# Loading half B's x^T in 320-column pieces, its decay products behind dense ones, cache set-up queued late, and half A's residual tiles at memory's other end, in a two-layer hybrid encoder step

## The chip, the cores and the metric

The kernel runs on one core of one Trainium2 chip. Its engines work side by side and each takes its own instructions in a fixed order: TensorE (PE, matrix products; PEld in the profile is its weight loading), VectorE (DVE), ScalarE (ACT), GpSimd (POOL) and SyncE (SP), which issues nearly all DMAs here. The metric is the device time of the program in microseconds (us). All arithmetic is fp32; a value x that enters a product is split into a rounded part hi and a rest lo, and a product is made as hi·hi + hi·lo + lo·hi, three matmuls.

## What is computed

The reference is one inference step of two layers over 1024 prompt frames and 64 sample frames of width 1024. Layer 0 projects x to the inputs of two mixers, a recurrent one (RWKV-7, 8 heads) and gated linear attention (GLA, 4 heads); layer 1 is chunk-band softmax attention that also reads a K/V cache of 128 rows. After each follow a layer norm, a SwiGLU channel mixer and another layer norm.

```python
for layer in range(DEPTH):
    if layer % 2 == 0:
        p = x @ P['w_in_mix'][e]
        ya, wkv, sh = rwkv7_time_mix(p[..., :A_PROJ], ...)
        yb, gs = gla_mix(p[..., A_PROJ:], gla0[e], P['b_alpha_up'][e], P['b_alpha_bias'][e], P['b_norm_w'][e])
        mix = jnp.concatenate([ya, yb], axis=-1) @ P['w_out_mix'][e]
    else:
        mix, kr, vr = chunk_band_attention(x, P['c_w_qkv'][o], P['c_rel_bias'][o], P['c_w_o'][o], ck, cv)
    x = layer_norm(DEEPNORM_ALPHA * x + mix, P['ln1_w'][layer], P['ln1_b'][layer])
    x = layer_norm(DEEPNORM_ALPHA * x + swiglu(x, P['ffn_w_in'][layer], P['ffn_w_out'][layer]), ...)
```

In gla_mix the decay is `log_sigmoid(xa @ alpha_up + alpha_bias) / 16`, where xa is 16 columns of the projection p.

## The kernel before

**Halves.** The tokens are cut in half A (hf = 0: 384 prompt frames and the 64 sample frames, 448 columns) and half B (hf = 1: the other 640 prompt frames). x is held transposed (x^T), as eight k tiles of 128 rows by the half's columns, each hi and lo.

**Order.** `run` (L1337) traces the program in an order; a scheduler then makes each engine's fixed order from it by a clock of its own: of the instructions that could go, the one traced first. So what is traced later serves as filler. Layer 0 runs like this: half A's input projection (`inproj_rwkv(0)`, `inproj_gla(0)`), then half A's recurrences (`rwkv(0)` and `gla(0)`, the scan below: many small matmuls and long chains of small DVE operations), with half B's input projection traced behind them, so that its dense products fill PE; then half B's scan, with half A's output projection, layer norm and ffn as filler.

**Half B's x^T.** At L1370 `xt_tiles_in` makes its tiles: the first three k tiles lie in tiles of their own (names xeh and xel, in a pool on the right end of memory), the other five lie over half A's x^T (names xh and xl), so they can be written only when half A's input projection has read what was there. `load_xt(1)` (L1371) loads each k tile [128, 640] into a buffer xraw of the tag wr, which has two buffers and is the one that all weights are loaded into (`load_w`, L94), casts it on ACT (L215) and subtracts on DVE or, for odd k tiles, POOL (L216). With a pool as argument, `load_xt` takes raw tiles yraw from that pool (tag yr, 8 buffers) instead; half A's loads do this with the pool yp.

**The projection of GLA.** `inproj_gla` (L339) first makes the decays: two loads (L344, L357), 16 products of 32 columns for each segment (L352, weights xaw), their evacuation (L355), then the up-projection (L363) and its functions, stored at L369. After that come four dense products for q and k (L370 to L377, each with 24 matmuls for each segment by `gemm_ws`, L124 to L126), then v (L382 to L388) and the gate (L389 to L397). Half B has two segments of 320 columns, half A one of 448.

**Memory.** Pools are stacked from the left or the right end. On the left, `yr` and `one` (buffers of the input projection) are closed at L1376 and L1378, and `ap` and `accA` come in their place: accA holds half A's residual tiles acc (`load_acc`, L793: four loads of 512 KB, L797) and the packed sample tile xpk (L851, L852). On the right lie the constants and the scan's pool, and on them the pool xb with xeh and xel, closed at L1376.

**Output projection of half A.** `load_xt(0, yg_d)` (L1377) reads the scans' outputs back into half A's x^T, k tile by k tile: 4 to 7 from GLA, 0 to 3 from RWKV, whose outputs y are stored at L654. `proj` (L855) multiplies first k tiles 4 to 7, then 0 to 3; the sums go to acc (L825, L827). It starts by packing the sample columns of all eight k tiles into xpk.

**Cache set-up.** `cache_setup` (L1117) is traced in half A's ffn, behind j = 8. It loads four parts of the V cache (tile cv, one buffer, L1122), casts them on ACT and subtracts on DVE (`split`, L113 and L114, tile cvh), and stores them (L1125); then the same for two parts of the K cache with a transpose on PE (L1128 to L1136). It depends on nothing before it, so the scheduler may put it anywhere earlier.

**Evacuation in the scan.** The scan's `rw1` makes three small products into the bank pa (L437 to L439), which ACT empties (L441, L443, L445); the next products pb (L484) need the same bank.

Of the kernel before, what the change touches and what calls it, by code (L numbers as in the profile page):

```python
# [20 lines left out]
NA, NB = PA + 64, 1024 - PA  # L21
NM = max(NA, NB)
# [61 lines left out]
class Kern:  # L84
# [9 lines left out]
    def load_w(self, src, shape):  # L94

        nc = self.nc
        raw = self.wp.tile(shape, F32, tag="wr", name="wr", bufs=2)
        self.last_w = nc.sync.dma_start(raw, src).ins
        hi = self.wp.tile(shape, F32R, tag="wh", name="wh", bufs=self.WB)
        lo = self.wp.tile(shape, F32R, tag="wl", name="wl", bufs=self.WB)  # L100
        self.A.copy(hi, raw)  # L101
        self.wcount += 1
        m = shape[1]
        h = m * 5 // 8 if self.both else m * (self.wcount % 2)
        if h:
            self.V.tensor_tensor(lo[:, :h], raw[:, :h], hi[:, :h].bitcast(F32), op=ALU.subtract)  # L106
        if h < m:
            self.G.tensor_tensor(lo[:, h:], raw[:, h:], hi[:, h:].bitcast(F32), op=ALU.subtract)  # L108
        return hi, lo
# [229 lines left out]
    def inproj_gla(self, hf, pool):  # L339
        nc, V, A, G, T = self.nc, self.V, self.A, self.G, self.T  # L340
        n, c0, xt = self.N[hf], self.base[hf], self.xt[hf]

        raw = pool.tile([128, 8, 16], F32, tag="xar", name="xar", bufs=1)
        nc.sync.dma_start(raw, self.a["w_xa"])  # L344
        whl = pool.tile([128, 8, 32], F32R, tag="xaw", name="xaw", bufs=1)
        A.copy(whl[:, :, 0:16], raw)
        V.tensor_tensor(whl[:, :, 16:32], raw, whl[:, :, 0:16].bitcast(F32), op=ALU.subtract)
        segs = self.banks(hf)
        for kt in range(8):
            for i, xx in enumerate((xt.h(kt), xt.l(kt))):  # L350
                for ps, s0, w in segs:
                    T.matmul(ps[0:32, :], whl[:, kt, :], xx[:, s0 : s0 + w], start=(kt + i == 0), stop=(kt + i == 8))  # L352
        xa = pool.tile([32, NM], F32, tag="xa", name="xa", bufs=1)
        for ps, s0, w in segs:
            V.tensor_copy(xa[:, s0 : s0 + w], ps[0:32, :])  # L355
        up = pool.tile([32, 256], F32, tag="up", name="up", bufs=1)
        nc.sync.dma_start(up, self.a["up2"])  # L357
        for p in range(2):
            segs = self.banks(hf)
            mn = pool.tile([128, NM], F32, tag="sq", name="mn", bufs=3)[:, :n]  # L360
            ab = pool.tile([128, NM], F32, tag="sq", name="abz", bufs=3)[:, :n]
            for ps, s0, w in segs:
                T.matmul(ps, up[:, 128 * p : 128 * p + 128], xa[:, s0 : s0 + w], start=True, stop=True)  # L363
                V.tensor_scalar(mn[:, s0 : s0 + w], ps, self.ab[:, p : p + 1], 0.0, op0=ALU.add, op1=ALU.min)
                A.activation(ab[:, s0 : s0 + w], ps, AF.Abs, bias=self.ab[:, p : p + 1])
            A.activation(ab, ab, AF.Exp, scale=-1.0)
            A.activation(ab, ab, AF.Ln, bias=self.one)
            G.tensor_tensor(ab, ab, mn, op=ALU.subtract)
            nc.sync.dma_start(self.qkl_d[2, p, :, c0 : c0 + n], ab)  # L369
        for ct in range(4):  # L370
            w = self.load_w(self.a["w_in"][14 + ct], [128, 8, 128])
            segs = self.banks(hf)
            self.gemm_ws(w, xt, segs)
            t = pool.tile([128, NM], F32, tag="t1", name="gq", bufs=2)
            for ps, s0, wd in segs:
                A.copy(t[:, s0 : s0 + wd], ps)
            nc.sync.dma_start(self.qkl_d[ct // 2, ct % 2, :, c0 : c0 + n], t[:, :n])  # L377
        ws = []
        for i in range(4):
            hi, lo = self.load_w(self.a["w_gv"][i], [128, 2, 512])  # L380
            ws += [(hi[:, 0, :], lo[:, 0, :]), (hi[:, 1, :], lo[:, 1, :])]
        for i0 in range(0, n, 128):  # L382
            m = min(128, n - i0)
            ps = self.bank()[:m]
            self.gemm_ts(ps, ws, xt.h, xt.l, list(range(8)), lambda x: x[:, i0 : i0 + m])
            t = pool.tile([128, 512], F32, tag="xs", name="gvs", bufs=2)
            A.copy(t[:m], ps)
            nc.sync.dma_start(self.gv_d[c0 + i0 : c0 + i0 + m, :], t[:m])  # L388
        for ct in range(4):  # L389
            w = self.load_w(self.a["w_in"][18 + ct], [128, 8, 128])  # L390
            segs = self.banks(hf)
            self.gemm_ws(w, xt, segs)
            t = pool.tile([128, NM], F32, tag="t1", name="grg", bufs=2)
            for ps, s0, wd in segs:
                A.activation(t[:, s0 : s0 + wd], ps, AF.Tanh, scale=0.5)
                V.scalar_tensor_tensor(t[:, s0 : s0 + wd], t[:, s0 : s0 + wd], 1.0, ps, op0=ALU.add, op1=ALU.mult)
            nc.sync.dma_start(self.sg_d[ct, :, c0 : c0 + n], t[:, :n])  # L397
# [939 lines left out]
    def run(self):  # L1337
        nc, tc, a = self.nc, self.tc, self.a
# [12 lines left out]
        yp = es_yr.enter_context(tc.tile_pool(name="yr", bufs=1))  # L1351
# [16 lines left out]
        for _ in g:  # L1368
            pass
        self.xt[1] = self.xt_tiles_in(es_one.enter_context(tc.tile_pool(name="xb", bufs=1, side="right")), 8 - NA * 8 // NB)  # L1370
        self.load_xt(1)  # L1371
        self.inproj_gla(1, one)
        self.inproj_rwkv(1, one)
        nc.sync.dma_start(a["s_shift"].rearrange("c p -> p c"), self.shS)
# [4 lines left out]

        self.ap = self.ctx.enter_context(tc.tile_pool(name="ap", bufs=1))  # L1380
        es_a = ExitStack()
        pa = es_a.enter_context(tc.tile_pool(name="accA", bufs=1))
        acc0 = self.load_acc(0, a["x"], pa)
        xd = lambda hf: (lambda t0, m: self.x_d[self.base[hf] + t0 : self.base[hf] + t0 + m, :])
        gS = []
# [16 lines left out]
        for j in self.ffn(0, 0, acc0, hp, lambda: self.layer_norm(0, acc0, "ln2", 0, xd(0))):  # L1402
            if j == 6:
                self.bias_setup(hp)
            if 12 <= j < 20:
                for h in range(2 * j - 24, 2 * j - 22):
                    self.bias_copies(h)
            if j == 8:
                with tc.tile_pool(name="as", bufs=1) as asp:
                    self.cache_setup(asp)  # L1410
        for p in range(4):
            self.wkv_out(sc, S[p], a["p_wkv"][2 * p : 2 * p + 2])
# [32 lines left out]
        accA = self.ctx.enter_context(tc.tile_pool(name="accA1", bufs=1, side="right"))  # L1445
# [7 lines left out]
        es_a = ExitStack()  # L1453
# [135 lines left out]
```

## Time and profile before

| what | us |
|---|---|
| median of 3 runs | 3117.12 |
| lowest, highest | 3116.71, 3119.89 |
| profiled execution | 3121.6 |
| its span, first to last instruction | 3119.8 |
| half B's x^T: first and last load issued | 151.3, 175.6 |
| V cache parts: first and last load issued | 532.0, 578.1 |
| K cache parts: loads issued | 584.9, 1005.8 |
| half A's residual tiles: first load issued | 562.3 |

In a row of stages stand the stretch and its length in us, then each engine's busy time with its instructions in brackets (PE, PEld, DVE, ACT, POOL, as far as they are asked for), then the granted clock of TensorE as a share of full speed, the share of time that the DMA engines are busy, and GB/s. A row of the order of time has start, duration, engine, line, operation, out<-in by the program's names, shapes and the number of instructions merged; in square brackets stands how long the engine was idle before it, and what ended that. SPq stands for DMAs that SP issues. A row of waits tells who waited for whom: sum in us, times, longest.

### The profile page before, as it was taken

The page shows a single profiled execution, that of the slowest core. Times are in us where ns is not written, and L with a number is a line of the kernel's source. Part 1 is how long each engine was busy: PE and PEld are TensorE (multiplying, and loading weights), DVE is VectorE, ACT ScalarE, POOL GpSimd, SP SyncE. Part 2 cuts the span into 40 slices and gives each one's busy share as a digit, 9 for nine tenths or more (in the row PEclk, how much of TensorE's full clock was granted, in tenths as well). Part 3 has the DMA queues.
Part 4 walks back from the last instruction along what each step waited for, and adds up shares of the span by engine and source line. Part 5 has one row for each costly group of instructions (what it writes and reads, how often), then busy time and mean ns, then how long its engine had stood idle before and what let it go on. Part 6 is the DMA issues. An engine that isn't in the chain of part 4 may idle for free. (4 is left out here: it accounts for less than half of the span.)

```text
span 3119.8 us, 50045 instructions
## 1 busy us (share of the span) xinstructions
PE 3017.0 (97%) x17468; PEld 2676.2 (86%) x17468; DVE 2021.3 (65%) x4941; ACT 1272.0 (41%) x2761; POOL 1363.5 (44%) x1489
## 2 busy tenths in 40 slices
PE   9999999899999999999999999999999989899998
PEld 7788888688888887888999899899999978799987
DVE  4677875879898764455554466245666667766567
ACT  4454554344454323233443132345444433333332
POOL 2354534444454333443332233244555555745444
PEclk9989999889999999999999999999999999999999
DMA  6554334533533228444343232866455443322222
GB/s 201 140 155 119 108 109 123 141 105 109 137 110 112 89 97 274 140 134 123 116 133 105 81 95 98 247 201 182 126 150 145 132 160 107 116 80 95 67 82 75
DMA packets 298492, 399.29 MB, mean 128 GB/s; under 512 B 125504, under 2 KB 218552, under 8 KB 298240
## 3 DMA queue, kind: packets, MB, share of 16 engines
q1 hardware_dynamic: 297088, 393.48, 42.4%
q8 instruction: 138, 2.26, 0.3%
q10 hardware_dynamic: 1152, 2.62, 0.2%
q14 instruction: 114, 0.93, 0.1%
HBM read 323.63 MB, written 75.51 MB: 128 GB/s over the span
## 5 line engine op out<-in xcount | busy, mean ns | idle before, releaser
L108 POOL TENSOR_TENSOR wl<-wr,wh 128x512 fp32r<-128x512 f32 (+2 forms) x297 | 521.7, 1760 | 642.1 <-ACT wh L101 592.3
L124 PE MATMUL gps<-xh,wh 128*128 128x320 f32 (+1 forms) x2188 | 746.0, 341 | 7.8 <-ACT xh L215 5.9
L125 PE MATMUL gps<-xl,wh 128*128 128x320 f32 (+1 forms) x2188 | 745.0, 340 | 0.6 <-DVE xl L216 0.6
L126 PE MATMUL gps<-xh,wl 128*128 128x320 f32 (+1 forms) x2188 | 744.3, 340 | 0.9 <-DVE wl L106 0.9
L101 ACT CAST wh<-wr 128x1024 fp32r<-128x1024 f32 x360 | 375.8, 1048 | 457.3 <-PE gps L125 131.2
L106 DVE TENSOR_TENSOR wl<-wr,wh 128x512 fp32r<-128x512 f32 (+2 forms) x297 | 289.6, 975 | 248.9 <-ACT wh L101 246.0
L124 PEld LDWEIGHTS gps<-xh,wh 128*128 128x128 f32 x2188 | 414.4, 189 | 30.6 <-ACT xh L215 5.9
L126 PEld LDWEIGHTS gps<-xh,wl 128*128 128x128 f32 x2188 | 413.8, 189 | 19.9 <-DVE wl L106 2.1
L125 PEld LDWEIGHTS gps<-xl,wh 128*128 128x128 f32 x2188 | 414.0, 189 | 18.1 <-DVE xl L216 1.0
L1294 POOL TENSOR_SCALAR s<-s,mx 128x640 f32<-128x640 f32 (+5 forms) x144 | 203.9, 1416 | 272.1 <-DVE mx L1293 250.7
L135 PE MATMUL gps<-wh,xh 128*128 128x512 f32 x661 | 262.0, 403 | 6.8 <-ACT xh L1092 2.5
L138 PE MATMUL gps<-wh,xl 128*128 128x512 f32 x661 | 258.9, 399 | 6.1 <-DVE xl L216 6.1
L136 PE MATMUL gps<-wl,xh 128*128 128x512 f32 x661 | 263.0, 400 | 1.3 <-DVE wl L106 1.1
L136 PE MATMUL gps<-wl,hh 128*128 128x512 f32 x572 | 226.7, 398 | 0.3 <-DVE wl L106 0.3
L135 PE MATMUL gps<-wh,hh 128*128 128x512 f32 x572 | 226.2, 397 | 0.3 <-DVE acc L827 0.3
L827 DVE TENSOR_TENSOR acc<-acc,gps 128x512 f32<-128x512 f32 x216 | 143.6, 679 | 86.8 <-PE gps L138 83.6
L138 PE MATMUL gps<-wh,hl 128*128 128x512 f32 x484 | 189.5, 398 | 2.2 <-DVE hl L942 2.2
L549 DVE TENSOR_TENSOR t<-lt,x 16x48 f32<-16x48 f32 (+9 forms) x540 | 147.3, 273 | 35.8 <-DMA lt<-l_d 25.4
L1292 ACT ACTIVATE s<-s,mx 128x640 f32<-128x640 f32 (+5 forms) x144 | 96.4, 669 | 162.3 <-DVE mx L1291 153.8
L135 PEld LDWEIGHTS gps<-wh,xh 128*128 128x128 f32 x661 | 125.9, 191 | 37.6 <-ACT wh L101 4.3
L138 PEld LDWEIGHTS gps<-wh,xl 128*128 128x128 f32 x661 | 125.7, 190 | 34.4 <-DVE xl L216 6.9
L136 PEld LDWEIGHTS gps<-wl,xh 128*128 128x128 f32 x661 | 126.2, 191 | 30.4 <-DVE wl L106 2.7
(383 smaller groups left out, 6327.8 us busy)
## 6 DMA issues: line engine op xcount, KB each, us to landing
wr<-in_w_fi SPq DMA_DIRECT2D x176, 512.0 KB
wr<-in_w_fo SPq DMA_DIRECT2D x88, 512.0 KB
wr<-in_w_in SPq DMA_DIRECT2D x44, 512.0 KB
wr<-in_w_qk SPq DMA_DIRECT2D x32, 512.0 KB
wr<-in_w_o SPq DMA_DIRECT2D x24, 512.0 KB
qs<-qd SPq DMA_DIRECT2D x32, 320.0 KB
wr<-in_w_om SPq DMA_DIRECT2D x16, 512.0 KB
wr<-in_w_v SPq DMA_DIRECT2D x16, 512.0 KB
```

What stands on the lines that cost most here:

```text
L101: self.A.copy(hi, raw)
L106: self.V.tensor_tensor(lo[:, :h], raw[:, :h], hi[:, :h].bitcast(F32), op=ALU.subtract)
L108: self.G.tensor_tensor(lo[:, h:], raw[:, h:], hi[:, h:].bitcast(F32), op=ALU.subtract)
L124: self.T.matmul(ps, hi[:, kt, :], xh, start=(kt == 0), stop=False)
L125: self.T.matmul(ps, hi[:, kt, :], xl, start=False, stop=False)
L126: self.T.matmul(ps, lo[:, kt, :], xh, start=False, stop=(kt == nk - 1))
L135: self.T.matmul(ps, xh, wh, start=(i == 0), stop=False)
L136: self.T.matmul(ps, xh, wl, start=False, stop=(lo is None and i == n - 1))
L138: self.T.matmul(ps, cols(lo(kt)), wh, start=False, stop=(i == n - 1))
L549: V.tensor_tensor(tv, lt[:, j, w:16].unsqueeze(2).to_broadcast([m, r, w]), x[:, 0, j, 0:w].unsqueeze(1).to_broadcast([m, r, w]), op=ALU.mult)
L827: self.V.tensor_tensor(a, a, ps[:m], op=ALU.add)
L1294: G.tensor_scalar(s[:m, :nk], s[:m, :nk], mx[:m, 3:4], None, op0=ALU.mult)
```

## The change

The casts of cache set-up are given an order behind the last weight cast traced so far (`last_cast`, set in `load_w`), and the cache's loads one behind the last weight load (`last_w`): `issue_after` puts every instruction that the block traces on that instruction's engine behind it. The decay products move into a function that half A calls where they stood and half B calls behind the four q and k products. Half B's x^T is loaded in 16 pieces of 320 columns through the pool yp. The pool accA goes to the right end.

```diff
-        self.A.copy(hi, raw)
+        self.last_cast = self.A.copy(hi, raw).ins
...
     def inproj_gla(self, hf, pool):
...
+        def decay():
+            raw = pool.tile([128, 8, 16], F32, tag="xar", name="xar", bufs=1)
+            nc.sync.dma_start(raw, self.a["w_xa"])
...
+                nc.sync.dma_start(self.qkl_d[2, p, :, c0 : c0 + n], ab)
+
+        if hf == 0:
+            decay()
         for ct in range(4):
             w = self.load_w(self.a["w_in"][14 + ct], [128, 8, 128])
...
             nc.sync.dma_start(self.qkl_d[ct // 2, ct % 2, :, c0 : c0 + n], t[:, :n])
+        if hf:
+            decay()
         ws = []
...
-        self.load_xt(1)
+        for kt in range(8):
+            for c in (0, NB // 2):
+                self.load_xt(1, None, (kt,), slice(c, c + NB // 2), yp)
         self.inproj_gla(1, one)
...
-        pa = es_a.enter_context(tc.tile_pool(name="accA", bufs=1))
+        pa = es_a.enter_context(tc.tile_pool(name="accA", bufs=1, side="right"))
...
-                with tc.tile_pool(name="as", bufs=1) as asp:
+                with tc.tile_pool(name="as", bufs=1) as asp, tc.issue_after(self.last_w), tc.issue_after(self.last_cast):
                     self.cache_setup(asp)
```

The body of `decay` is what stood at the head of `inproj_gla` before, unchanged.

More of the change, by code (lines that the diff above doesn't have):

```diff
@@ L341, in inproj_gla @@
         n, c0, xt = self.N[hf], self.base[hf], self.xt[hf]
[L343 to L350, printed above, removed]
-                for ps, s0, w in segs:
-                    T.matmul(ps[0:32, :], whl[:, kt, :], xx[:, s0 : s0 + w], start=(kt + i == 0), stop=(kt + i == 8))
@@ L353, in inproj_gla @@
[L353 to L369, printed above, removed]
+        def decay():
+            raw = pool.tile([128, 8, 16], F32, tag="xar", name="xar", bufs=1)
+            nc.sync.dma_start(raw, self.a["w_xa"])
+            whl = pool.tile([128, 8, 32], F32R, tag="xaw", name="xaw", bufs=1)
+            A.copy(whl[:, :, 0:16], raw)
+            V.tensor_tensor(whl[:, :, 16:32], raw, whl[:, :, 0:16].bitcast(F32), op=ALU.subtract)
+            segs = self.banks(hf)
+            for kt in range(8):
+                for i, xx in enumerate((xt.h(kt), xt.l(kt))):
+                    for ps, s0, w in segs:
+                        T.matmul(ps[0:32, :], whl[:, kt, :], xx[:, s0 : s0 + w], start=(kt + i == 0), stop=(kt + i == 8))
+            xa = pool.tile([32, NM], F32, tag="xa", name="xa", bufs=1)
+            for ps, s0, w in segs:
+                V.tensor_copy(xa[:, s0 : s0 + w], ps[0:32, :])
+            up = pool.tile([32, 256], F32, tag="up", name="up", bufs=1)
+            nc.sync.dma_start(up, self.a["up2"])
+            for p in range(2):
+                segs = self.banks(hf)
+                mn = pool.tile([128, NM], F32, tag="sq", name="mn", bufs=3)[:, :n]
+                ab = pool.tile([128, NM], F32, tag="sq", name="abz", bufs=3)[:, :n]
+                for ps, s0, w in segs:
+                    T.matmul(ps, up[:, 128 * p : 128 * p + 128], xa[:, s0 : s0 + w], start=True, stop=True)
+                    V.tensor_scalar(mn[:, s0 : s0 + w], ps, self.ab[:, p : p + 1], 0.0, op0=ALU.add, op1=ALU.min)
+                    A.activation(ab[:, s0 : s0 + w], ps, AF.Abs, bias=self.ab[:, p : p + 1])
+                A.activation(ab, ab, AF.Exp, scale=-1.0)
+                A.activation(ab, ab, AF.Ln, bias=self.one)
+                G.tensor_tensor(ab, ab, mn, op=ALU.subtract)
+                nc.sync.dma_start(self.qkl_d[2, p, :, c0 : c0 + n], ab)
@@ L1370, in run @@
         self.xt[1] = self.xt_tiles_in(es_one.enter_context(tc.tile_pool(name="xb", bufs=1, side="right")), 8 - NA * 8 // NB)
-        self.load_xt(1)
+        for kt in range(8):
+            for c in (0, NB // 2):
+                self.load_xt(1, None, (kt,), slice(c, c + NB // 2), yp)
         self.inproj_gla(1, one)
```

## The prediction

> **What bounds the kernel now.** I read the page's totals first, then the table of stages, then, inside the two stages that lose time, the order of time of single engines.
>
> ```profile
> span 3119.8 us, 50045 instructions
> PE 3017.0 (97%) x17468; PEld 2676.2 (86%) x17468; DVE 2021.3 (65%) x4941; ACT 1272.0 (41%) x2761; POOL 1363.5 (44%) x1489
> ```
>
> PE is busy 97% of the span, so the others matter only where they hold it up, or where it runs at the lower granted clock. The table of stages (length, then busy time and instructions of each engine, then granted clock, DMA share, GB/s) shows where that is.
>
> ```profile
> 0.00:30.00 30.00, 22.64 (x87) 17.91 (x88) 13.30 (x33) 14.18 (x20) 6.57 (x11) 1.00 0.78 253
> 84.00:98.50 14.50, 11.37 (x40) 6.92 (x39) 7.58 (x25) 8.58 (x25) 6.53 (x15) 0.77 0.74 110
> 168.50:177.00 8.50, 6.96 (x50) 5.19 (x49) 4.49 (x8) 4.17 (x14) 3.37 (x6) 1.00 0.52 157
> 177.00:200.90 23.90, 23.58 (x93) 17.34 (x94) 17.86 (x62) 14.02 (x37) 15.78 (x31) 0.50 0.45 140
> 200.90:530.00 329.10, 323.21 (x2288) 287.50 (x2288) 250.35 (x896) 164.94 (x488) 139.23 (x257) 0.99 0.42 119
> 535.20:583.20 48.00, 33.16 (x150) 27.20 (x149) 32.22 (x94) 17.26 (x53) 19.58 (x30) 0.79 0.72 169
> 583.20:611.40 28.20, 28.00 (x150) 22.55 (x150) 27.83 (x69) 9.17 (x22) 12.14 (x14) 1.00 0.33 88
> 611.40:645.00 33.60, 27.70 (x135) 21.83 (x133) 29.29 (x75) 15.31 (x45) 22.74 (x29) 0.54 0.38 118
> 645.00:1160.00 515.00, 511.46 (x3091) 438.58 (x3089) 416.76 (x1273) 221.78 (x616) 225.44 (x343) 0.99 0.38 107
> 800.00:880.00 80.00, 78.89 (x503) 67.02 (x502) 68.91 (x229) 37.67 (x117) 38.58 (x63) 0.98 0.46 125
> ```
>
> Two stages stand out. From 177.0 to 200.9 PE is busy 23.58 of 23.90 us, at half clock throughout. From 535.2 to 583.2 it is busy 33.16 of 48.00 us at 0.79. Between and after them PE is nearly full at 0.99 (329.10 and 515.00 us), so a shift won in either stage should be carried through them; 611.4 to 645.0 is the layer norm of half A, where DVE has 29.29 of 33.60 us, and should move as a block.
>
> **Part one: x^T of half B, and the decay products.** The order of time on PE, and the waits of the tile xraw:
>
> ```profile
> 168.32 0.37 PE L126 MATMUL gps<-xh,wl 128*128 128x448 f32 x1
> 169.92 0.47 PE L352 MATMUL gps<-xeh,xaw 128*32 128x320 f32 x2
> 185.30 0.88 PE L352 MATMUL gps<-xl,xaw 128*32 128x320 f32 x2
> 198.11 0.64 PE L124 MATMUL gps<-xeh,wh 128*128 128x320 f32 x1
> ...
> L214 SPq DMA_DIRECT2D xraw<-in_xt x8: 333/340/432, 151.3 to 175.6; - x8
> L215 ACT CAST xh<-xraw x5: 712/725/728, 166.3 to 178.6; 128x640 fp32r<-128x640 f32 x5
>   DMA xraw<-in_xt: 10.9, 7
> ```
>
> Half A's last dense product ends at 168.7. From 169.92 PE has only the thin decay products (32 columns of the array) and the scan's small ones until the first dense one at 198.11. The decay products take from 169.92 to 186.2 because the eight loads of x^T pass two buffers that the weights also use: the last is issued at 175.6, and the casts waited 10.9 us for landings, seven times. After the change the loads have eight buffers of their own, and dense products come first. Of the 16 pieces six go to the separate tiles xeh, xel and can be split early; ten lie over half A's x^T and become writable as its last product passes (it ends at 168.7). Ten casts at half of 0.725 us are 3.6 us of ACT; the first dense segment takes 24 x 0.15 = 3.6 us (0.15 from one such matmul to the next, rows 531.47 and 531.62 further down) and the scan's products stand between, so I count no wait of PE there.
>
> The gain: 23.9 us at half clock become 12.0 if dense products are mixed in, and the idle 8.50 - 6.96 = 1.5 us go: 13.5. What comes back: the decay products still run, and half A's did so in the row 84.00:98.50, with 14.50 - 11.37 = 3.1 us idle and 0.23 x 14.5 = 3.3 us of clock. With dense v products of half B ready beside them I take 3.0 of those 6.4. **Term one: -10.5**, from -13.5 to 0.
>
> The Trainium skill (TensorE: Matmul & The Clock Gate, "What's actually happening") has full clock return after one busy window of about 3.4 us. Here PE was busy for 23.58 us and stayed at 0.50, so the trace disagrees. By that rule the slow stretch would have ended after 3.4 us whatever the products were, and mixing in dense ones would win next to nothing.
>
> Eight more issues on SP (0.34 us each) are 2.7 us among idle ones. The loads may now be issued as soon as the buffers are free, since a half-B load is issued early already:
>
> ```profile
> 31.48 0.37 SPq L344 DMA_DIRECT2D xar<-in_w_xa  x1
> ...
> PE gps L124 <- ACT wh L101: 0.9, 1, 0.9
> ```
>
> Eight pieces of 128 x 320 x 4 bytes are 1.31 MB, 5.2 us at the 253 GB/s of the first 30 us, whose DMA share is 0.78 and where PE waited 0.9 us once for a weight. **Term two: +1.0**, from 0 to 5.2, nearer to the one wait seen.
>
> The Trainium skill (DMA: Bandwidth & Descriptors, "Rules for kernel authors") wants 1 MiB or more per DMA and speaks against pieces of 160 KB. No row here prices a piece of that size; eight in flight should hide it.
>
> **Part two: cache set-up out, residual tiles on the right.** The order of time of SP, ACT, DVE and PE, and one row of SP's waits:
>
> ```profile
> 543.02 0.51 SPq L303 DMA_DIRECT2D rkv_d<-xs  x1
> 553.91 0.36 SPq L427 DMA_DIRECT2D rkv<-rkv_d  x1
> 554.37 0.44 SPq L654 DMA_DIRECT2D yg_d<-y  x1
> 555.37 0.43 SPq L1122 DMA_DIRECT2D cv<-in_ck_v  x1
> 558.43 0.32 SPq L214 DMA_DIRECT2D yraw<-yg_d  x1
> 562.34 1.82 SPq L797 DMA_DIRECT2D acc<-in_x  x4
> ...
> SPq L427 <- DMA rkv_d<-xs: 8.0, 1, 8.0
> ...
> 544.80 0.47 POOL L653 TENSOR_TENSOR y<-y,gt 128x128 f32<-128x128 f32 x1
> 559.77 0.41 ACT L113 CAST cvh<-cv 128x256 fp32r<-128x256 f32 x1 [12.26 <-DMA cv<-in_ck_v]
> 562.53 0.77 POOL L852 CAST xpk<-xl 128x512 fp32r<-128x512 f32 x1
> 566.89 0.67 DVE L825 SCALAR_TENSOR_TENSOR acc<-acc,gps 128x512 f32<-128x512 f32 x1
> 531.47 0.31 PE L125 MATMUL gps<-xel,wh 128*128 128x320 f32 x1
> 531.62 0.30 PE L126 MATMUL gps<-xeh,wl 128*128 128x320 f32 x1
> 560.91 2.08 PE L484 MATMUL pb<-ar,bbk 128*128 128x128 f32 x8 [8.44 <-ACT gt L445]
> 568.21 0.80 PE L135 MATMUL gps<-wh,xpk 128*128 128x512 f32 x1
> ...
> 560.90:568.20 7.30, 5.73 (x26) 5.13 (x26) 6.71 (x23) 4.02 (x13) 3.59 (x8) 0.50 0.77 262
> ...
> PE pt L509 <- DVE arb L497: 1.6, 1, 1.6
> ...
> L114 DVE TENSOR_TENSOR cvh<-cv,cvh x4: 404/416/426, 541.7 to 583.6; 128x256 fp32r<-128x256 f32 x4
> ```
>
> SP stood 8.0 us until 553.9 for rkv_d. Behind it came the third load of the V cache (cv); ACT, which works in order, stood 12.26 us in front of that load's cast, and PE 8.44 us for the evacuation queued behind it. The residual tiles (acc) were loaded only at 562.34, because their place on the left overlaps the buffers of the x^T pieces, the last of which was loaded at 558.43; so the first acc sum came at 566.89 and PE's next output projection at 568.21. After the change the cv loads come in the ffn, and acc, now over xeh and xel, can be loaded from 531.9, where PE last reads them. What is late next is the packed tile xpk: it needs the last y (ready at 545.3, sent at 554.37 after SP's wait for rkv_d, which nothing here removes), and POOL ends it at 563.3. If that stays, PE goes on at 563.3 and not 568.2: 4.9 us won. If the order lets other products go ahead, 8.4 us of idle go, the 1.6 us in front of pt, and half of the 5.7 us that PE was busy at half clock after 560.9 (row 560.90:568.20): 12.9. **Term three: -7.0**, from -12.9 to 0, nearer to 4.9, whose row is a hand-over that stays.
>
> Cache set-up itself is moved: four casts of 0.41 us and as many DVE splits, and eight DMA issues, to about 800 to 880 us. There ACT has 37.67 of 80 us, so it fits; if its cover goes, ACT stands in front of each cast again, and the scan's evacuations and the weight casts wait behind it, and PE for them. The K half follows its bank as before. **Term four: +1.0**, from 0 to the slower rival's price.
>
> Sum: -10.5 + 1.0 - 7.0 + 1.0 = -15.5. The profiled execution took 3121.6 us (span 3119.8 and 1.8 around it), so 3106.1; the median of the runs is 4.5 lower than it: **3101.6**.
>
> **The rivals.** *Scan A sets the end*: its last y, ready at 545.3, comes from a chain of small operations, and if that chain does not move when dense work does, PE only arrives earlier and waits. For: DVE has 250.35 of 329.10 us there, in order. Against: PE has 323.21, and waits little. Term one goes; -7 + 2 = -5 leaves 3112. The same holds if dense work doesn't keep the clock up. *All of it*: -13.5 - 12.9 and no cost is -26: 3091. *It doesn't do what it says*: the scheduler orders by its own clock, and x^T may still arrive after 168.7 and xpk still gate: 3117, give or take 3. *Slower*: the cv loads land late in the ffn too, and ACT stands in front of their casts. Price of one: the 8.4 us of idle and some 3.4 of slow clock behind it, as after the wait above; 11.8. One is paid by the gain; from two of four (+23.6) on it decides: 3101.6 + 23.6 = 3125. For: a single buffer, SP in order. Against: one of four did it before, behind rkv_d.
>
> **How the numbers follow.** Forecast 0.43 (its own range 3094 to 3110), scan A 0.22, all of it 0.13, nothing 0.08, slower 0.14. A difference of 0.2% (6.2 us) is about what can be told from no change: below 3110.9 is faster, above 3123.4 slower. The scan case straddles the first bound (0.11 of it faster). So faster 0.67, same 0.19, slower 0.14. The range, with the bounds of the terms and most of the other cases, is 3086 to 3122.
>
> **What would show it.** Right: dense L124 on xeh directly after half A's last product, no half clock for the next 30 us, decay products after the four q and k products; no cvh cast before the ffn; acc loaded before 550; the bunch of layer norm operations that now starts at 611.4 some 15 us earlier. Wrong: PE idle between half A's and half B's products; the last y at 545 and PE waiting for xpk; ACT idle over 5 us in front of cvh; PE waiting for weights before 40 us.

## The result, and the profile after

The changed kernel took 3126.21 us (median of 9 runs, 3122.65 to 3136.11) beside 3116.71 for the kernel before (9 runs, 3112.76 to 3120.61): a ratio of 1.0031, 95% interval 1.0023 to 1.0040. It is slower by 0.3%; the forecast was 3101.6, and its range ended at 3122.

The profiled executions show a third of this. The changed kernel's took 3124.67 (1.5 under its median), the one of the kernel before 3121.6 (4.9 over its own): 3.1 of the 9.5 us. Single executions of one kernel differ by 8 us (before) and 13 us (changed), so a cause that only two profiles show is weak; what follows uses the profiles of twenty kernels. First the totals of the changed kernel.

```profile
span 3122.9 us, 50128 instructions
PE 3007.6 (96%) x17468; PEld 2670.3 (86%) x17468; DVE 2009.6 (64%) x4945; ACT 1272.0 (41%) x2769; POOL 1360.7 (44%) x1493
```

PE does the same 17468 products and is busy 9.4 us less, yet the span is longer: PE idles 115.3 us instead of 102.8, so what was gained in clock went into idle time. The table of stages of the changed kernel (columns as in the prediction) shows where:

```profile
162.50:171.50 9.00, 9.00 (x53) 8.40 (x52) 5.87 (x8) 6.08 (x15) 5.49 (x4) 1.00 0.52 162
171.50:200.50 29.00, 27.95 (x199) 25.36 (x198) 22.25 (x75) 14.24 (x48) 18.50 (x34) 1.00 0.38 122
220.00:240.40 20.40, 19.49 (x111) 15.00 (x109) 14.59 (x58) 15.60 (x35) 9.54 (x21) 1.00 0.41 117
526.00:564.00 38.00, 20.93 (x93) 16.91 (x92) 20.52 (x67) 11.52 (x39) 12.15 (x21) 0.69 0.57 110
639.00:1156.00 517.00, 513.87 (x3091) 439.98 (x3092) 410.17 (x1264) 222.85 (x619) 219.95 (x342) 0.98 0.38 110
```

Part one did what was forecast: from 171.5 to 200.5 PE is busy 27.95 of 29.00 us at full clock, where the kernel before had 23.9 us at half. The order of time on PE, and the instructions of line L353 (the decay products, L352 before; after the colon their shortest, median and longest time in ns, then the start of the first and the last in us), show the new order:

```profile
169.35 0.41 PE L124 MATMUL gps<-xeh,wh 128*128 128x320 f32 x1
```

```profile
L353 PE MATMUL gps<-xeh,xaw x6: 304/309/312, 213.1 to 216.5; 128*32 128x320 f32 x6
L353 PE MATMUL gps<-xl,xaw x10: 304/309/337, 219.1 to 221.6; 128*32 128x320 f32 x10
```

The output projection's start, 526 to 564, is as bad as before: 20.93 of 38.00 us busy, at 0.69.

To compare kernels whose orders differ I count the dense products (L124 to L126 and L135 to L138 of the kernel before; 10712 in every kernel) and take the start of the k-th, counted from 0. In the table, the kernel before in us and the others as differences from it. The 640th lies in half B's first dense products, the 1800th at the start of half A's output projection, the 1976th is the first of half A's ffn, the 3512th the ffn's end, and from the 3690th to the 3760th PE goes over to the q and k products of the attention.

| k | before | changed | xd_only | null_product | null_after_2 | before_flat |
|---|---|---|---|---|---|---|
| 640 | 201.8 | -30.0 | -27.2 | -2.6 | -27.5 | -0.3 |
| 1000 | 304.2 | -6.9 | -3.1 | +0.6 | -4.9 | -0.7 |
| 1800 | 535.2 | -9.3 | -1.3 | +11.1 | -0.2 | -0.5 |
| 1840 | 569.8 | -5.7 | +0.1 | +7.1 | -9.4 | -7.4 |
| 1976 | 639.2 | -0.4 | +4.7 | +15.0 | -2.1 | -6.8 |
| 2600 | 865.5 | +8.1 | +12.0 | +11.8 | +1.6 | -8.9 |
| 3512 | 1159.0 | -2.9 | +1.0 | +6.8 | -7.0 | -8.4 |
| 3690 | 1215.2 | -2.3 | -0.3 | +9.5 | -6.3 | -8.3 |
| 3760 | 1231.4 | +2.5 | +0.8 | +16.3 | -4.1 | -8.5 |
| 10700 | 3104.6 | +3.1 | +5.1 | +17.6 | -3.6 | -6.0 |

In the changed kernel a gain of 9.3 us at the 1800th product is gone by the 1976th; 4.8 more go at the switch to the attention. The bulge to +8.1 at the 2600th product comes back: from the 1840th to the 2600th PE has 1746 records instead of 1684, and from there to the 3512th 1675 instead of 1751, so scan work that was done earlier is missing later.

**The hole near 545.** Waits of the changed kernel from 535 to 560 (engine, tile, line, who it waited for: sum, times, longest), the same for SyncE, then its order of time on SyncE and on VectorE. Its line numbers run 6 on from the projection (L831 is L825 of the kernel before).

```profile
DVE acc L831 <- DMA acc<-in_x: 13.8, 1, 13.8
ACT eb L461 <- DVE b L459: 11.2, 1, 11.2
PE gpa L731 <- DVE gy L764: 10.9, 1, 10.9
...
SPq L803 <- DMA rkv_d<-xs: 9.3, 1, 9.3
```

```profile
532.53 0.34 SPq L303 DMA_DIRECT2D rkv_d<-xs  x1
532.97 0.39 SPq L1383 DMA_DIRECT2D out_dram<-shP  x1
533.45 1.81 SPq L98 DMA_DIRECT2D wr<-in_w_om  x1
544.65 1.29 SPq L803 DMA_DIRECT2D acc<-in_x  x3
546.03 0.38 SPq L660 DMA_DIRECT2D yg_d<-y  x1
```

```profile
551.40 0.69 DVE L831 SCALAR_TENSOR_TENSOR acc<-acc,gps 128x512 f32<-128x512 f32 x1 [13.78 <-DMA acc<-in_x]
552.62 0.41 DVE L459 TENSOR_TENSOR_SCAN b<-m,lw 128x130 f32<-128x130 f32 x1
```

No cache cast stands in the hole any more; the first residual sum does. VectorE, in order, stood 13.78 us in front of it, with the scan's operation b behind it, ScalarE behind b, and PE 10.9 us behind both. The residual loads went out at 544.65, after SyncE had stood 9.3 us, by the profile for the rkv_d store. The waiting instruction is new; the hole is no smaller (8.44 us of PE before).

**Layer norm and switch.** Two stages each of the kernel before and of the changed one: from the 1900th to the 1976th dense product, and from the 3690th to the 3760th.

```profile
586.90:639.20 52.30, 46.20 (x236) 36.78 (x234) 50.32 (x120) 20.84 (x55) 30.48 (x38) 0.76 0.35 102
1215.20:1231.40 16.20, 15.04 (x72) 12.92 (x71) 13.08 (x13) 11.07 (x17) 13.24 (x8) 1.00 1.02 343
```

```profile
579.60:638.80 59.20, 49.24 (x256) 38.94 (x254) 54.86 (x140) 22.62 (x63) 33.94 (x41) 0.76 0.32 99
1212.90:1233.90 21.00, 16.42 (x72) 14.22 (x72) 11.57 (x13) 11.78 (x16) 13.75 (x12) 0.92 0.92 323
```

VectorE is the bound of the first stage: 50.32 of 52.30 us busy, 54.86 of 59.20 after. It is not a block that moves: the scheduler put 140 VectorE records there instead of 120, so PE, with only the scan's products to do, idles longer (52.30 - 46.20 = 6.1 us before, 10.0 after). In the second stage PE waits for the first weight cast of q and k:

```profile
1218.13 0.74 PE L124 MATMUL gps<-xh,wh 128*128 128x448 f32 x1 [4.58 <-ACT wh L101]
```

In the kernel before, the same product waited 0.39 us.

### The profile page after: what moved, and what is told of

The parts are those of the page before. It is cut to its first block, busy times and chain, and to the rows that moved or that the text cites. A ratio compares the mean times of both kernels' runs of the same rounds, so it can differ in the third digit from the quotient of the medians.

```text
span 3122.9 us, 50128 instructions
## 1 busy us (share of the span) xinstructions
PE 3007.6 (96%) x17468; PEld 2670.3 (86%) x17468; DVE 2009.6 (64%) x4945; ACT 1272.0 (41%) x2769; POOL 1360.7 (44%) x1493
## 5 line engine op out<-in xcount | busy, mean ns | idle before, releaser
L124 PE MATMUL gps<-xh,wh 128*128 128x320 f32 (+1 forms) x2188 | 749.8, 343 | 13.7 <-ACT wh L101 6.7
L126 PE MATMUL gps<-xh,wl 128*128 128x320 f32 (+1 forms) x2188 | 747.2, 342 | 0.0
L124 PEld LDWEIGHTS gps<-xh,wh 128*128 128x128 f32 x2188 | 416.6, 191 | 37.5 <-ACT wh L101 8.3
L126 PEld LDWEIGHTS gps<-xh,wl 128*128 128x128 f32 x2188 | 416.2, 190 | 18.2 <-DVE wl L106 0.4
L135 PE MATMUL gps<-wh,xh 128*128 128x512 f32 x661 | 262.5, 403 | 8.2 <-ACT wh L101 4.2
L138 PE MATMUL gps<-wh,xl 128*128 128x512 f32 x661 | 259.4, 399 | 5.2 <-DVE xl L216 5.2
L135 PE MATMUL gps<-wh,hh 128*128 128x512 f32 x572 | 226.2, 397 | 0.3 <-DVE acc L833 0.3
L138 PE MATMUL gps<-wh,hl 128*128 128x512 f32 x484 | 187.7, 395 | 0.0
L555 DVE TENSOR_TENSOR t<-lt,x 16x48 f32<-16x48 f32 (+9 forms) x540 | 132.8, 246 | 42.5 <-DMA lt<-l_d 31.9
L135 PEld LDWEIGHTS gps<-wh,xh 128*128 128x128 f32 x661 | 125.9, 191 | 38.6 <-ACT wh L101 6.3
L138 PEld LDWEIGHTS gps<-wh,xl 128*128 128x128 f32 x661 | 125.7, 190 | 33.6 <-DVE xl L216 6.1
```

What stands on the lines that cost most here:

```text
L124: self.T.matmul(ps, hi[:, kt, :], xh, start=(kt == 0), stop=False)
L126: self.T.matmul(ps, lo[:, kt, :], xh, start=False, stop=(kt == nk - 1))
L135: self.T.matmul(ps, xh, wh, start=(i == 0), stop=False)
L138: self.T.matmul(ps, cols(lo(kt)), wh, start=False, stop=(i == n - 1))
L555: V.tensor_tensor(tv, lt[:, j, w:16].unsqueeze(2).to_broadcast([m, r, w]), x[:, 0, j, 0:w].unsqueeze(1).to_broadcast([m, r, w]), op=ALU.mult)
```

## The experiments

Each ratio is to the kernel before, run on the same chip beside it, with its 95% interval. The kernel before took 3116.67 to 3123.44 us on these chips, so only ratios are compared from kernel to kernel. "Lost" is PE's idle time and half of its busy time at half clock, from the profiled execution.

| kernel | ratio | lost to the 1800th | lost 1800th to 4400th | 1900th to 1976th | 3690th to 3760th |
|---|---|---|---|---|---|
| before | 1 | 37.3 | 68.3 | 52.3 | 16.2 |
| changed | 1.0031 | 25.8 | 80.5 | 59.2 | 20.9 |
| xd_only | 1.0018 | 36.1 | 70.3 | 57.8 | 17.3 |
| x_only | 1.0027 | 36.5 | 68.3 | 57.6 | 22.5 |
| c_only | 1.0035 | 29.2 | 76.1 | 54.0 | 23.1 |
| r_only | 1.0058 | 40.5 | 84.3 | 59.0 | 20.1 |
| cr_only | 1.0058 | 37.1 | 80.6 | 58.2 | 20.1 |
| before_flat | 0.9980 | 37.4 | 63.3 | 51.9 | 16.0 |
| after_flat | 1.0008 | 35.2 | 70.5 | 57.4 | 21.0 |
| before_transposed | 1.0020 | 34.5 | 80.2 | 80.3 | 23.7 |
| null_product | 1.0075 | 49.0 | 73.8 | 59.2 | 23.0 |
| null_before_2 | 1.0069 | 41.1 | 74.8 | 53.4 | 22.5 |
| null_before_3 | 1.0046 | 31.8 | 82.3 | 58.7 | 24.4 |
| null_after_1 | 1.0046 | 34.7 | 71.9 | 55.7 | 15.6 |
| null_after_2 | 1.0002 | 33.0 | 64.3 | 57.0 | 18.4 |
| null_after_3 | 1.0037 | 40.5 | 75.6 | 55.1 | 15.6 |

### The halves of the change

xd_only is the kernel before with part one (x^T in pieces, decay products behind dense ones); cr_only with part two (cache set-up late, residual tiles on the right). Of the diff shown above each leaves the other half out.

> The kernel before plus part one alone: half B's x^T in pieces and its decay products behind the q and k products; cache set-up and the residual tiles stay as before. Theory H (part one works as forecast, what was lost was lost in part two): the dense product on xeh comes right after half A's last one, near 169, the long half clock from 177 to 201 is gone, the k-th dense product comes some 9 us earlier up to 526, and the hole near 550 stays as in the kernel before; 3116.7 - 9 = about 3108, between 3104 and 3112. Rival L (the gain of part one is swallowed later whatever part two does, by the hand-over to the output projection and the layer norm, which wait for something that does not move): earlier by 9 at 526, by less than 3 at 680, and 3117 give or take 3.

Measured: 3124.86 us, 1.0018 (1.0010 to 1.0027). Theory H had 9 us at the 1800th product; there were 1.3. Theory L was nearer, but its 3117 give or take 3 (0.9990 to 1.0011 of the kernel before) ends below the measured ratio, and it had the place wrong: the gain was gone before the output projection. xd_only has the same order on every engine as the changed kernel up to 524 us, so this is one order executed twice. Stages of xd_only, then its order of time on PE:

```profile
171.50:200.50 29.00, 27.47 (x193) 24.68 (x194) 23.41 (x74) 15.26 (x49) 20.09 (x33) 1.00 0.39 126
220.00:240.40 20.40, 18.02 (x83) 13.28 (x84) 13.31 (x51) 12.18 (x33) 7.90 (x18) 0.75 0.38 107
```

```profile
221.16 0.33 PE L621 MATMUL ps<-rr,btt 64*64 64x64 f32 x2 [1.20 <-DVE btt L593]
227.01 0.41 PE L583 MATMUL pz<-tt,lab 128*128 128x64 f32 x2 [1.21 <-DMA tt<-s_d]
```

The long half clock is gone here too, but near where the decay products now stand PE waited 1.20 and 1.21 us, and the clock fell for 10.2 us; the changed kernel's profile has these two waits with 1.07 and 0.91 us, and full clock in its row from 220.0 to 240.4. The waits alone don't decide it: after_cast_first has 1.20 and 0.46 us with that half clock, after_all_mended 1.24 and 0.41 without it.

Five executions of this one order (changed, after_flat, xd_only, after_cast_first, and after_all_mended, in which only the stores of the shift rows differ up to there) had the 1800th product at -9.3, -1.1, -1.3, +0.1 and -5.6. The order of the kernel before was executed six times to some 530 us: before, before_flat and before_via_dram had the product at 0, -0.5 and -1.9, and c_only, r_only and cr_only, whose orders part from it only behind 531 us, at -5.8, +2.2 and -1.1. The means, -3.44 and -1.18, are 2.3 us apart, with a standard error of 2.1. So the 9.3 us of the changed kernel's profile are the best of five draws. The half clock of the kernel before is a draw as well: in its six executions the stretch that begins between 175 and 189 us lasted 23.9, 27.3, 23.9, 10.2, 17.1 and 23.9 us.

> The kernel before plus part two alone: cache set-up queued behind the ffn's weights, residual tiles on the right; x^T and decay as before. By the prediction's own steps (cv gone from 535 to 583, acc loaded early): 3117 - 7 + 1 = 3111. Theory H: the hole near 550 is only handed from the cache cast on ScalarE to the first residual sum on VectorE, which waits over 8 us for its load, and the cache set-up costs some 4 us in the ffn: 3120 to 3126. The theories part at 3116.

Measured: 3138.48, 1.0058 (1.0044 to 1.0073), more than theory H allowed, and against the sign of the prediction's term.

### The wake of the single floats

```diff
-        nc.sync.dma_start(a["p_shift"].rearrange("c p -> p c"), self.shP)
+        nc.sync.dma_start(a["p_shift"].rearrange("c p -> (c p)").rearrange("(p c) -> p c", p=128), self.shP)
```

> The kernel before with one store changed: p_shift goes out as 128 rows of 14 neighbouring floats instead of 1792 single floats (the numbers of p_shift land in another order; nothing else reads them). Theory S: the hole near 550 is the wake of these single floats, in which the other transfers of 4096 bytes a packet take 1 to 2 us each instead of 0.18. Then the weight load behind it moves at once, SyncE's wait of 8.0 us for rkv_d and ScalarE's of 12.26 for cv shrink below 3, PE's idle of 8.44 us below 2, and the time is 8 to 12 us lower: 3105 to 3109, down to 3112 if a part is lost later. Rival C: the cache part and its single buffer make the hole: same hole, 3117 give or take 2.

> The changed kernel with the same store as 128 rows of 14 floats (the numbers of p_shift land in another order). Theory S: the residual loads' wait of 9.3 us on SyncE and VectorE's of 13.8 us in front of the first residual sum shrink to under 5, PE's 10.9 us of idle near 543 go, and the time is 8 to 15 us lower than the changed kernel's: 3111 to 3118. Rival A: the first residual sum is queued too early on VectorE whatever the store does, and waits for 2 MB of loads: 3123 to 3128.

before_flat: 3114.40, 0.9980 (0.9971 to 0.9990). It leaves p_shift's numbers in another order than the reference, so it serves to measure only, as after_flat does. Every other instruction has the place it had before, on every engine and to the end, so this is the cleanest of the experiments. The transfers in 7 us behind that store, of the kernel before (547 to 554) and of before_flat (546 to 553): packets, megabytes, and their time as a share of 16 engines.

```profile
DMA packets 180, 0.27 MB, mean 39 GB/s; under 512 B 114, under 2 KB 114, under 8 KB 180
...
q1 hardware_dynamic: 180, 0.27, 97.1%
```

```profile
DMA packets 1741, 1.37 MB, mean 196 GB/s; under 512 B 633, under 2 KB 1525, under 8 KB 1741
...
q1 hardware_dynamic: 1741, 1.37, 68.0%
```

In the kernel before, the DMA engines were busy 97.1% of the time with 180 packets: 7 x 16 x 0.971 / 180 = 0.60 us each. In before_flat it is 7 x 16 x 0.68 / 1741 = 0.04 us. The packets are not of the same sizes, but those of 4096 bytes can be compared: the 66 of the kernel before took 1.58 us in the median, the 85 of before_flat 0.16. The 1792 single floats of p_shift hold up whatever is behind them for some 8 us. The order of time of before_flat on SyncE, PE and ScalarE:

```profile
546.86 0.37 SPq L427 DMA_DIRECT2D rkv<-rkv_d  x1
...
553.23 1.16 PE L484 MATMUL pb<-ar,bbk 128*128 128x128 f32 x8 [1.87 <-ACT gt L445]
...
552.09 0.41 ACT L113 CAST cvh<-cv 128x256 fp32r<-128x256 f32 x1 [5.72 <-DMA cv<-in_ck_v]
```

SyncE goes on at 546.86 instead of 553.91, PE's hole shrinks from 8.44 to 1.87 us, and the 7 us stay to the end of the ffn (-8.4 at the 3512th product), 6.0 to the end. The cache cast still waits 5.72 us for its load; it was in the hole, but did not make it. Theory S has the hole, and the time at the far end of what it allowed (0.9980 of 3116.7 is 3110.5, up to 3112); of its signs only ScalarE's wait stayed over 3 us. Rival C falls.

after_flat: 3122.11, 1.0008 (0.9999 to 1.0017), 0.23% below the changed kernel. VectorE's wait of 13.8 us is no longer among its long waits in that stretch. Theory S expected 3111 to 3118, 0.9982 to 1.0004 of the kernel before; the ratio is a little above, and below rival A's (from 1.0020).

### One part at a time

```diff
-        self.load_xt(1)
+        for kt in range(8):
+            for c in (0, NB // 2):
+                self.load_xt(1, None, (kt,), slice(c, c + NB // 2), yp)
```

That is x_only; c_only has the two issue_after alone, r_only only side="right".

> The kernel before plus the late cache set-up alone. Theory S (the wake of the single-float store near 545 holds whatever waits for a transfer there): with no cv cast in ScalarE's queue the hole near 550 shrinks but something else that waits for a load stands there; in the ffn the casts and splits and the loads that stand among the weights cost some 4 us (the changed kernel lost 4.5 between 832 and 873). Together 0.999 to 1.002 of the kernel before. Rival P (the prediction's term: hole gone, 1 us given back): 0.9975 to 0.9985. Rival B (late cache set-up is the whole cause of the slower time of both parts): 1.003 to 1.006.

> The kernel before plus the residual tiles on the right alone. Theory Q: their loads get a wait for the half-B tiles' readers and land late, the first residual sum waits for them on VectorE with the scan's operations behind it (13.8 us in the changed kernel, and PE idle 10 to 12), and near 1213 the switch to half B's x^T costs some 4 us more: 1.002 to 1.005 of the kernel before. Rival P (the prediction's term: the tiles are loaded early and PE goes on 5 us earlier): 0.998. If neither c_only nor r_only is slower by 0.2%, the 0.58% of both together comes from their meeting in one order, not from a part.

> The kernel before plus half B's x^T in pieces alone; the thin decay products stay in front of the dense ones. Theory L (what is won near 170 to 200 is given back before 530): the decay products are fed sooner, so PE's idle between 168 and 200 goes, the half clock there stays near 20 us, 2 to 3 us at 210, nothing at the end: 0.999 to 1.001. Rival D (the order of the decay products costs what part one loses later, through the scan's waits behind them at 220 to 240): here 0.997 to 0.999, since the pieces gain and the decay products stay.

c_only 3130.57, 1.0035 (1.0021 to 1.0049); r_only 3140.94, 1.0058 (1.0046 to 1.0071); x_only 3130.95, 1.0027 (1.0017 to 1.0038). x_only lies outside what either of its theories allowed, and r_only above theory Q's; c_only lies in rival B's range, but r_only, without the late cache set-up, is slower still. Waits of c_only from 535 to 565, then of r_only from 545 to 575:

```profile
PE pt L512 <- DVE t L552: 10.8, 1, 10.8
ACT xh L215 <- DMA yraw<-yg_d: 8.6, 1, 8.6
```

```profile
DVE acc L828 <- DMA acc<-in_x: 12.4, 2, 12.1
PE gpa L728 <- DVE gy L761: 8.4, 1, 8.4
```

With the cache casts away, the cast of the read-back x^T (yraw) stands in the wake, and PE idles 10.8 us; with the residual tiles on the right it is their sum. Each placement finds another instruction for the same wake. But all five partial kernels are slower, each part alone included, and the last two columns of the table show the same two places in nearly all of them: 20 to 23 us instead of 16.2 at the switch (17.3 in xd_only), 54 to 59 instead of 52.3 in the layer norm. None of the parts works at the switch.

### Orders that only differ

null_product adds one product that nothing reads, ahead of half B's x^T; null_before_2 has it ahead of half B's RWKV projection, null_before_3 ahead of half A's GLA projection. null_after_1, 2 and 3 are the changed kernel with the same three edits.

```diff
+        jps = self.bank()
+        self.T.matmul(jps[:, 0:128], self.ident, self.ident, start=True, stop=True)
```

> The kernel before plus one product of 128 x 128 (0.1 us) ahead of half B's x^T, into a bank that nothing reads; nothing of the change. It makes the scheduler set all five orders anew from there. Theory Z (most of the loss is not of the parts: any new order loses at two places, where the one before stood well): ScalarE has four casts of half B's read-back x^T ahead of the first weight cast at the switch near 1215 (the kernel before: two), so PE stands there 4 us longer; VectorE has 61 instead of 53 small inverse steps between the first residual sum and the end of the layer norm, 2 us: 1.001 to 1.003 of the kernel before. Rival P (the loss is of the parts): 0.9990 to 1.0008, and the stretch of the 70 dense products round 1215 stays at 16 us instead of 20 to 23.

> The kernel before plus one product of 128 x 128 that nothing reads, this time ahead of half B's RWKV projection. Theory Z (a new order costs by itself, and the kernel before stands at the good end of its own possible orders): 1.002 to 1.006 of the kernel before, with 20 to 24 us for the 70 products round 1215 (16.2 before) and 53 to 56 us from the 1900th to the 1976th dense product. Rival P (null_product was an exception; the loss of the changed kernel is its parts' own): 0.999 to 1.001.

> The same product ahead of half A's GLA projection. Theory Z: 1.002 to 1.006. Rival P: 0.999 to 1.001.

> The changed kernel plus the product of null_product at the same place. Theory Z: anywhere from 1.002 to 1.007 of the kernel before, no further from it than the null edits of the kernel before are. Rival P: 1.002 to 1.004, like the changed kernel itself, and above the null edits of the kernel before by 0.2% or more.

> The changed kernel plus the product of null_before_2 at the same place. Theory Z: 1.002 to 1.007, within 0.15% of null_before_2 or below it. Rival P: 1.002 to 1.004 and 0.2% or more above null_before_2. Both theories: 57 to 60 us from the 1900th to the 1976th dense product, since the residual sums stand early in VectorE's order in every kernel with the tiles on the right (72 to 84 inverse steps against 53 to 61).

> The changed kernel plus the product of null_before_3 at the same place: the third pair. Theory Z with a gain of the parts' own (the two pairs so far: 1.0046 against 1.0075, 1.0002 against 1.0069): 0.1% to 0.6% below null_before_3's 1.0046, so 0.9990 to 1.0036. Theory Z without one: 1.0046 give or take 0.002, either side. Rival P: over 1.0060.

| dead product | in the kernel before | in the changed kernel | difference |
|---|---|---|---|
| none | 1 | 1.0031 (1.0023 to 1.0040) | +0.31% |
| ahead of half B's x^T | 1.0075 (1.0059 to 1.0090) | 1.0046 (1.0030 to 1.0062) | -0.29% |
| ahead of half B's RWKV | 1.0069 (1.0056 to 1.0081) | 1.0002 (0.9993 to 1.0010) | -0.67% |
| ahead of half A's GLA | 1.0046 (1.0032 to 1.0059) | 1.0037 (1.0025 to 1.0050) | -0.09% |

Such an edit, called a null edit from here on, adds next to no work and changes the orders behind it. A dead product of 0.1 us costs 0.46 to 0.75%, 14 to 23 us, more than the whole change and, twice, more than theory Z expected: all five engines get a new order behind it. (It also takes one of three banks out of turn.) In the changed kernel the same three products cost +0.15, -0.29 and +0.06%, so the price is not the product's own: it depends on the order that the product meets. Rival P falls: the null edits of the kernel before lie above the changed kernel, not at 1.000. null_after_2 lies below what either theory allowed, and null_after_3 excludes rival P (over 1.0060) but decides nothing between the two forms of theory Z. Over the four pairs the change is worth (+0.31 - 0.29 - 0.67 - 0.09) / 4 = -0.19%, with a standard error of 0.20% from their spread: a gain of its own is not shown, nor a loss. The kernel before stands at the low end of the orders drawn. The two places of the last columns are not the whole price: null_after_1 and null_after_3 have 15.6 us at the switch and are slower all the same. Two stages of null_product, cut as above:

```profile
595.00:654.20 59.20, 47.25 (x249) 38.70 (x248) 56.17 (x141) 22.41 (x59) 28.49 (x39) 0.77 0.36 109
1224.70:1247.70 23.00, 17.59 (x72) 15.24 (x71) 13.20 (x14) 11.68 (x17) 13.66 (x8) 0.85 0.88 288
```

Both losses of the changed kernel, 59.2 us in the layer norm and over 20 at the switch, are here without any part of the change.

### Mending the places

before_transposed turns both shift rows on PE and stores them as 14 rows:

```diff
+        for dst, sh in ((a["s_shift"], self.shS), (a["p_shift"], self.shP)):
+            ps = self.sbank("tps")
+            self.T.transpose(ps[:14, 0:128], sh, self.ident)
...
+            self.A.copy(row, ps[:14, 0:128])
+            nc.sync.dma_start(dst, row)
```

> The kernel before with s_shift and p_shift transposed on PE (one 128 x 14 product and one evacuation each) and stored as 14 rows of 512 bytes, all outputs as in the reference. Theory S: no transfer crawls near 547 to 555 or near 92 to 98; SyncE's wait of 8.0 us and PE's idle of 8.44 go as with before_flat, and 2 to 4 us near 92; 0.997 to 0.998 of the kernel before, if the new order brings nothing of its own, which may add or take 0.1%. Rival: only the order differs: 0.999 to 1.001.

Measured: 3128.22, 1.0020 (1.0010 to 1.0029), a miss. The hole went (23.4 us from the 1800th to the 1840th product, 34.6 before), but the new order put far more of the scan in the layer norm, and its row shows VectorE bound for 80 us:

```profile
574.60:654.90 80.30, 64.67 (x333) 53.07 (x331) 70.66 (x207) 29.27 (x88) 40.66 (x62) 0.68 0.33 91
```

after_cast_first puts the read-back casts of half B behind the weight casts (`with tc.issue_after(self.last_cast)` round that load_xt).

> The changed kernel with one order added: the casts of half B's read-back x^T near 1210 stand behind the last weight cast traced so far, so the weights of the q and k products are cast first. Other orders hardly move. Theory Z: PE's idle of 4.58 us at 1213.6 falls below 1, the 3.4 us of half clock behind it go, and the kernel is 4 to 6 us faster than the changed one: 1.0012 to 1.0020 of the kernel before. Rival W (PE waits for the loads there, not for the order of the casts): the idle stays or moves a few us on, 1.0025 to 1.0035.

Measured: 3140.73, 1.0055 (1.0040 to 1.0070), 0.24% above the changed kernel. Rival W was right about the wait, and its time too low. The order of time of after_cast_first on ScalarE, SyncE and PE:

```profile
1224.37 0.59 ACT L113 CAST vh<-gps 128x512 fp32r<-128x512 f32 x1 [11.19 <-DMA vd<-vh]
1224.86 1.99 ACT L101 CAST wh<-wr 128x1024 fp32r<-128x1024 f32 x2
...
1213.90 2.70 SPq L214 DMA_DIRECT2D yraw<-yg_d  x6
1216.70 0.38 SPq L1220 DMA_DIRECT2D vd<-vh  x1
...
1225.96 0.74 PE L124 MATMUL gps<-xh,wh 128*128 128x448 f32 x1 [5.02 <-ACT wh L101]
```

The weight casts do come first, but a cast of v ahead of them waits for a store (vd) that SyncE issued behind six read-back loads. PE idles 5.02 us instead of 4.58. That the order of the casts makes this wait is refuted; here it is the store behind those loads.

before_via_dram stores the shift rows to DRAM scratch as 128 rows where the single-float stores stood, and scatters them from there in layer 1, behind the last weight load; PE, VectorE, ScalarE and GpSimd have the order of the kernel before throughout. after_all_mended has that and the reordered casts; after_2_via_dram is null_after_2 with it.

```diff
-        nc.sync.dma_start(a["p_shift"].rearrange("c p -> p c"), self.shP)
+        nc.sync.dma_start(self.psh_d, self.shP)
...
+            with tc.issue_after(self.last_w):
+                nc.sync.dma_start(a["p_shift"].rearrange("c p -> p c"), self.psh_d)
```

> The kernel before with s_shift and p_shift stored first as 128 rows of 56 bytes to scratch memory in DRAM, where the single-float stores stood, and scattered from there in layer 1, behind the attention's first loads; all outputs as in the reference, and every engine's order up to the attention as before. Theory S: like before_flat, no crawl near 547, 0.9975 to 0.9985 of the kernel before, with up to 2 us more from s_shift near 92. Rival: the wake only moves, and costs the same in the attention: 0.9995 to 1.0005.

> The changed kernel with both mendings: shift rows by way of DRAM, and the read-back casts behind the weight casts. If the losses add up, 1.0031 - 0.0023 (the wake, as after_flat against the changed kernel) - 0.0015 (the switch near 1215) = 0.9993 of the kernel before, 0.9985 to 1.0002, and 4 to 6 us behind before_via_dram, which would be what the layer norm's longer queue on VectorE (72 against 53 inverse steps) and the start take. Rival: part one's gain of 9 us comes through once nothing else is in its way: under 0.9975.

> null_after_2 (1.0002) with the two shift rows by way of DRAM, as in before_via_dram. If the wake's price adds to any order: 1.0002 - 0.0014 to 0.0023 = 0.998 to 0.999, level with before_via_dram's 0.9986. Theory Z: the store's place changes the order behind it once more, and the new draw weighs more than the wake: anywhere from 0.998 to 1.004.

before_via_dram: 3116.64, 0.9986 (0.9977 to 0.9995), at the upper end of theory S and below its rival. after_all_mended: 3124.57, 1.0010 (0.9997 to 1.0023), a little above what was expected. after_2_via_dram: 3118.02, 0.9985 (0.9976 to 0.9994), 0.17% below null_after_2 and within what the wake's price alone would give, though its order differs again. before_via_dram and after_2_via_dram are faster than both the kernel before and the changed one.

## Why the prediction was wrong

**The step that failed** is "so a shift won in either stage should be carried through them", and with it that the layer norm "should move as a block". The sum priced the stages that the change touches and held the rest fixed. But an edit gives every engine a new order from there on, and the kernel before had a better one than any of its three null edits: these cost 0.46 to 0.75%, 14 to 23 us. No term stood for that, and it is as large as the forecast gain of 15.5 us. From the 1800th to the 1976th dense product the changed kernel lost 8.9 us against the kernel before, and after_cast_first, which has the same order there, 9.8. The layer norm did not move as a block: its first statistics on VectorE (L883) start at 584.4 instead of 591.4, its last at 623.0 instead of 627.6, not 15 us earlier. All other signs that the prediction named for being right came out, and the time did not: they watch the places that were touched.

**Term one (-10.5): the mechanism was right, the size was not.** Dense products come at 169.35, right behind half A's last; the decay products stand at 213.1 to 221.9, behind q and k; there is no half clock from 171.5 to 200.5. In the profiled execution the 1800th product was 9.3 us early. But -10.5 was mis-sized: over five executions of the new order and six of the old one the mean gain at that product is 2.3 us, with a standard error of 2.1, and the 9.3 were luck. Two figures in it were single draws. The old half clock, 23.9 us in the profile, lasted 10.2 to 27.3 us, 21.1 in the mean; and the 3.0 us put down for the decay products' return were too few, since in three of the five executions a new half clock of 10.2 us began at 228 to 231, 4 to 5 us behind them (5.1 us, and waits). Which wait or product lets the clock fall is open. The Trainium skill (TensorE: Matmul & The Clock Gate, "What's actually happening") calls the activity window free-running, so that one kernel differs from run to run. The traces agree: one order, with that half clock in three executions and without it in two. Its rule that 3.4 busy us bring the full clock back fits none of the six executions of the old order, if time filled with records is busy: in r_only PE's records fill 17.10 of 17.10 us (183.2 to 200.3) at 0.50.

**Term two (+1.0)** can't be told from the spread: the 100th dense product came 2.8 us later in the changed kernel, but 2.3 later in before_flat, which has none of it.

**Term three (-7.0) had the wrong sign.** It took the cache load for the cause of the hole, where the profile showed only which instruction stood in it. It also had "acc, now over xeh and xel, can be loaded from 531.9"; they went out at 544.65, and VectorE stood 13.78 us for the first. PE took up the packed tile xpk at 563.18, as forecast (563.3), but that was no gain: the stretch from the 1800th to the 1840th product took 38.3 us instead of 34.6 (38.1 in after_cast_first). Some 7 us were there to be won, but by the store: the kernel before takes 27.6 us for this stretch in before_flat and 28.8 in before_via_dram. That "nothing here removes" SyncE's wait was true and should have been followed to its cause.

**Term four (+1.0)** is open: c_only lies within the spread of the null edits. In the changed kernel the cache casts come near 832 to 852, and ScalarE waited little for them (waits from 800 to 860):

```profile
ACT cvh L113 <- DMA cv<-in_ck_v: 6.1, 3, 3.0
```

**The rivals.** *Scan A sets the end* is refuted: its last y was ready at 534.9 instead of 545.3, moving with the dense work. *Slower*, 3125, had the time by luck: it wanted waits of over 8 us for cv in two of four casts, and the longest is 3.0. Of *It doesn't do what it says* one half came true: xpk still gated, at 563.18, while x^T was there in time.

## What to carry to other kernels

An instruction named in a wait is the one that stood there, not the cause: look at what the DMA engines did meanwhile, and undo the suspect with every order kept. Where a scheduler sets the orders, draw the spread of null edits first; a change worth less than that spread can only be judged over several pairs.

## What the runs showed of the hardware

A store of 1792 single floats (7 KB) made other transfers crawl for some 8 us: 1.58 us for a packet of 4096 bytes in the median instead of 0.16, with the DMA engines 97.1% busy at 39 GB/s. As 128 rows of 56 bytes it left no such wake. The Trainium skill (DMA: Bandwidth & Descriptors, "Rules for kernel authors") says that a strided last dimension becomes one descriptor per element and should be made contiguous; the runs agree, with 1710 packets of 4 bytes from 545 to 547 us (18 in before_flat), and show that the price falls on the transfers behind. How the one does this to the other no run shows. Scattered from DRAM in the attention instead (before_via_dram), its price can't be told: 0.9986 against 0.9980 for before_flat, which never scatters, with intervals that overlap.

The granted clock differs between executions of one order on every engine: the half clock near 180 us lasted 10.2 to 27.3 us in six executions, and the one near 230 us was there in three executions of five.
